# A float32 column sum: all loads but the first moved to the gpsimd queue, with shrinking tiles and a left-then-right end

## The chip, the cores and the metric

The kernel runs on one core of a Trainium2 chip. The metric is the device time of one execution in microseconds. Executions of one kernel beside each other lie within 0.3% here (630.0 to 630.8 us for the kernel before); only `tail_only` spreads by 0.5% (639.4 to 642.3 us). So differences of 2 us or more are safe here, and differences below 1 us are only called a tie or a tendency.

The engines are called as in the profile: PE is the tensor engine (PEld its weight loads), DVE the vector engine, ACT the scalar engine, POOL the gpsimd engine, SP the sync engine. A "queue" is the engine that issues a load. Loads issued by SP show up in the profile as `hardware_dynamic`, loads issued by POOL as `software_dynamic`.

## The reference

```python
# grad_output: (32, 1024, 2048) float32
def reference(grad_output):
    return np.sum(grad_output, axis=(0, 1)).astype(np.float32)     # 2048 sums over 32768 rows
```

The input is 268.4 MB and is read once. Below, a "row" is a slab of 128x2048 floats (1 MiB, one input row in each of the 128 partitions); there are 256 of them.

## The kernel before

31 tiles of 8 rows are loaded into three buffers. DVE folds each tile in halves (8 rows to 4 to 2 to 1) and adds the result to `acc`. The last 8 rows go into one more tile of the same three buffers, in pieces, and are not folded: PE multiplies them, and also `acc`, with a column of ones, which sums over the partitions into PSUM. The 2048 columns are cut into five pieces; the third number of a piece picks PSUM rows 0, 32, 64 or 96, called its row group here.

```python
ROWS = 8
TAIL = (4, 2, 1)
PIECES = ((0, 512, 1), (512, 512, 2), (1024, 512, 3), (1536, 256, 0), (1792, 256, 0))
# ... pools: io_pool with bufs=3, one tile of 128 x 8*2048 floats each; ones; acc ...
    for b, (lo, n, g) in enumerate(PIECES):
        bank = psum_pool.tile([P, 512], fp32, tag=f"ps{b}", name=f"ps{b}")
        sums.append(bank[32 * g : 32 * g + 1, :n])
# ...
    for t in range(n_bulk):                                   # 31 tiles
        T = io_pool.tile([P, ROWS * D], fp32, tag="T", name=f"t{t}")
        nc.sync.dma_start(out=T[:], in_=src)
        n = ROWS * D // 2
        while n >= D:                                         # 8 -> 4 -> 2 -> 1 rows
            # (the last step of tile 0 writes acc)
            nc.vector.tensor_add(out=T[:, :n], in0=T[:, :n], in1=T[:, n : 2 * n])
            n //= 2
        if t:
            nc.vector.tensor_add(out=acc[:], in0=acc[:], in1=T[:, :D])
    T = io_pool.tile([P, ROWS * D], fp32, tag="T", name="tail")
    for i, m in enumerate(TAIL):                              # 4, 2, 1 rows, then matmuls
        nc.sync.dma_start(out=T[:, at * D : (at + m) * D], in_=src)
        # ... add_row(...) for each of the m rows
    add_row(acc[:])
    for b, (lo, n, g) in enumerate(PIECES):                   # the last row, in five loads
        nc.sync.dma_start(out=dst, in_=flat[row : row + P, lo : lo + n])
        add_piece(b, dst, stop=True)
        # copy sums[b] to res: ACT for b = 0, 2, 4, DVE for b = 1, 3
    nc.sync.dma_start(out=out[None, :], in_=res)
```

The instruction streams are not simply this text. The build puts each engine's instructions in an order of its own, as the data dependencies allow.

## Time and profile before

| | before |
|---|---|
| time, median of 3 (630.2 us of 4 in the result below) | 630.1 us |
| span of the profiled run | 628.2 us |
| DMA: share of 16 engines' span | 99.0% |
| DVE busy | 87% |
| adds of one 8-row tile | 8.69 + 4.43 + 2.29 + 2.29 = 17.7 us |
| from tile to tile | 19.4 us |
| first adds start | 22.6 us |

From the profile page of the kernel before: the DMA share in 40 slices of the span, the rate in the same slices, and the queue.

```profile
DMA  9999999999999999999999999999999999999996
GB/s 401 413 455 401 467 401 467 401 467 401 467 401 467 401 467 401 463 405 459 409 459 409 455 413 455 413 455 413 451 417 451 417 446 421 438 430 426 442 403 266
q1 hardware_dynamic: 5618, 268.45, 99.0%
```

The DMA engines are busy in every slice but part of the last. (The rates swing because a packet, of which one of 64 KB takes 2.43 us on the mean in this trace, is counted whole in the slice where it starts.) This kernel is bound by its loads.

The groups of DVE instructions, kept apart by shape: count, total busy us, mean ns, and the idle time before them.

```profile
L67 DVE TENSOR_TENSOR t<-t 128x8192 f32<-128x8192 f32 x31 | 269.5, 8692 | 71.8 <-DMA t<-in_grad_output_dram 71.8
L67 DVE TENSOR_TENSOR t<-t 128x4096 f32<-128x4096 f32 x31 | 137.2, 4425 | 1.1
L70 DVE TENSOR_TENSOR acc<-acc,t 128x2048 f32<-128x2048 f32 x30 | 68.8, 2292 | 1.0
```

DVE waits for a load before every tile (71.8 us in all). The timeline of DVE at the start: start us, duration us, instructions (merged where they follow on).

```profile
22.61 13.15 DVE L67 TENSOR_TENSOR t<-t 128x8192 f32<-128x8192 f32 x2 [21.76 <-DMA t<-in_grad_output_dram]
35.80 2.29 DVE L65 TENSOR_TENSOR acc<-t 128x2048 f32<-128x2048 f32 x1
41.97 15.48 DVE L67 TENSOR_TENSOR t<-t 128x8192 f32<-128x8192 f32 x3 [3.88 <-DMA t<-in_grad_output_dram]
```

Tile 0 is folded from 22.6 to 38.1 us, and its buffer is then free for the fourth load. The three loads issued at the start keep the DMA engines busy until about 60.9 us, where their last packets end in the trace (their first packets start at 1.8 us). So the fourth load has over 20 us to spare.

The end, in windows of half a microsecond (the columns are busy us of PE, PEld, DVE, ACT, POOL, then clock, DMA share, GB/s), and the last wait for a landing, the copies and the store in the timeline:

```profile
622.00:622.50 0.50, 0.50 (x13) 0.26 (x9) 0.24 (x1) 0.00 (x0) 0.00 (x0) 1.00 1.06 361
622.50:623.00 0.50, 0.50 (x13) 0.26 (x8) 0.00 (x0) 0.00 (x0) 0.00 (x0) 1.00 0.57 182
623.00:623.50 0.50, 0.50 (x11) 0.09 (x2) 0.00 (x0) 0.00 (x0) 0.00 (x0) 1.00 0.07 25
```
```profile
624.20 0.20 PEld L49 LDWEIGHTS ps<-tail,ones 128*1 128x1 f32 x2 [0.24 <-DMA tail<-in_grad_output_dram]
624.34 1.57 ACT L89 COPY acc<-ps 1x512 f32<-1x512 f32 x3 [622.12 <-PE ps L49]
624.38 1.13 DVE L91 COPY acc<-ps 1x512 f32<-1x512 f32 x2 [2.14 <-PE ps L49]
625.93 0.33 SPq L92 DMA_DIRECT2D out_dram<-acc  x1
```

Traffic, counted where packets start, ends at about 622.7 us, the three ACT copies run one after another, and the store ends the span at 628.2: 5.5 us after 622.7.

### The profile page before, as it was taken

To read this page: it belongs to the slowest core of one execution; us is meant where nothing else is said; L and a number is where in the kernel's file an instruction comes from. 1 tells how busy PE (TensorE), PEld (TensorE's weight loads), DVE (VectorE), ACT (ScalarE), POOL (GpSimd) and SP (SyncE) were. 2 spreads that over 40 slices of the span, in tenths; PEclk is the share of its full clock that TensorE was granted. 3 is DMA by queue.
4 is the path that set the end of the run, shared out by engine and by line. 5 is a ranking of instruction groups with operands and counts; after the bars stand their busy time and mean duration, and the time that the engine had idled before them with its cause. 6 is when DMAs were issued, how large, how long until landed. Compare 5 with 4: busy or idle time off the path is not lost.

```text
span 628.2 us, 430 instructions
## 1 busy us (share of the span) xinstructions
PE 10.6 (2%) x90; PEld 3.8 (1%) x90; DVE 547.6 (87%) x126; ACT 3.0 (0%) x5; POOL 0.2 (0%) x4
## 2 busy tenths in 40 slices
PE   0000000000000000000000000000000000000006
PEld 0000000000000000000000000000000000000002
DVE  0578988889888899888898888988889988899886
ACT  0000000000000000000000000000000000000000
POOL 0000000000000000000000000000000000000000
PEclk9999999999999999999999999999999999999999
DMA  9999999999999999999999999999999999999996
GB/s 401 413 455 401 467 401 467 401 467 401 467 401 467 401 467 401 463 405 459 409 459 409 455 413 455 413 455 413 451 417 451 417 446 421 438 430 426 442 403 266
DMA packets 5619, 268.45 MB, mean 427 GB/s; under 512 B 625, under 2 KB 881, under 8 KB 1265
## 3 DMA queue, kind: packets, MB, share of 16 engines
q1 hardware_dynamic: 5618, 268.45, 99.0%
q14 instruction: 1, 0.01, 0.0%
HBM read 268.44 MB, written 0.01 MB: 427 GB/s over the span
## 4 chain that ended last, share of the span: by engine, by line
DMA 69%; DVE 28%; PE 2%; issue 0%; ACT 0%; SPq 0%; ACTq 0%
DMA t<-in_grad_output_dram 64%; DVE t L67 25%; DMA tail<-in_grad_output_dram 5%; DVE acc L70 4%; PE ps L49 2%; ACT acc L89 0%; SPq L60 0%; ACTq L118 0%
## 5 line engine op out<-in xcount | busy, mean ns | idle before, releaser
L67 DVE TENSOR_TENSOR t<-t 128x8192 f32<-128x8192 f32 (+2 forms) x92 | 475.4, 5167 | 73.9 <-DMA t<-in_grad_output_dram 71.8
L70 DVE TENSOR_TENSOR acc<-acc,t 128x2048 f32<-128x2048 f32 x30 | 68.8, 2292 | 1.0
L49 PE MATMUL ps<-tail,ones 128*1 128x512 f32 (+1 forms) x80 | 10.0, 627 | 614.3 <-DMA tail<-in_grad_output_dram 614.3
L49 PEld LDWEIGHTS ps<-tail,ones 128*1 128x1 f32 x80 | 3.5, 97 | 620.3 <-issue 617.4
L89 ACT COPY acc<-ps 1x512 f32<-1x512 f32 (+1 forms) x3 | 1.5, 506 | 622.2 <-PE ps L49 622.1
L91 DVE COPY acc<-ps 1x512 f32<-1x512 f32 (+1 forms) x2 | 1.1, 548 | 2.2 <-PE ps L49 2.1
L65 DVE TENSOR_TENSOR acc<-t 128x2048 f32<-128x2048 f32 x1 | 2.3, 2292 | 0.0
L39 ACT ACT_TABLE_LOAD x1 | 1.3, 1283 | 0.7 <-PEq L107 0.7
L49 PE MATMUL ps<-acc,ones 128*1 128x512 f32 (+1 forms) x10 | 1.1, 507 | 0.0
L37 DVE MEMSET ones<- 128x1 f32 x1 | 0.1, 59 | 0.8 <-PEq L107 0.8
L49 PEld LDWEIGHTS ps<-acc,ones 128*1 128x1 f32 x10 | 0.4, 82 | 0.4 <-DVE acc L70 0.2
L39 ACT COPY warm<-ones 1x1 f32<-1x1 f32 x1 | 0.2, 190 | 0.0
L107 POOL MEMSET const-bfloat16-1.0<- 128x1 bf16 x1 | 0.1, 101 | 0.0
L107 POOL MEMSET const-uint8-127<- 128x1 uint8 x1 | 0.1, 101 | 0.0
L107 POOL MEMSET const-float32-0.0<- 128x1 f32 x1 | 0.1, 98 | 0.2 <-issue 0.2
L107 POOL MEMSET const-float32-1.0<- 128x1 f32 x1 | 0.1, 98 | 0.0
## 6 DMA issues: line engine op xcount, KB each, us to landing
tail<-in_grad_output_dram SPq DMA_DIRECT2D x1, 4096.0 KB
tail<-in_grad_output_dram SPq DMA_DIRECT2D x1, 2048.0 KB, 35.1
tail<-in_grad_output_dram SPq DMA_DIRECT2D x1, 1024.0 KB, 37.1
tail<-in_grad_output_dram SPq DMA_DIRECT2D x3, 256.0 KB, 37.5
t<-in_grad_output_dram SPq DMA_DIRECT2D x31, 40.2
tail<-in_grad_output_dram SPq DMA_DIRECT2D x2, 128.0 KB, 28.6
out_dram<-acc SPq DMA_DIRECT2D x1, 8.0 KB
```

Source lines behind the costliest of these rows:

```text
L37: nc.vector.memset(ones[:], 1.0)
L39: nc.scalar.copy(out=warm[:], in_=ones[0:1, :])
L49: nc.tensor.matmul(sums[b], lhsT=ones[:], rhs=src, start=(b not in started), stop=stop)
L65: nc.vector.tensor_add(out=acc[:], in0=T[:, :n], in1=T[:, n : 2 * n])
L67: nc.vector.tensor_add(out=T[:, :n], in0=T[:, :n], in1=T[:, n : 2 * n])
L70: nc.vector.tensor_add(out=acc[:], in0=acc[:], in1=T[:, :D])
L89: nc.scalar.copy(out=res[:, lo : lo + n], in_=sums[b])
L91: nc.vector.tensor_copy(out=res[:, lo : lo + n], in_=sums[b])
L107: nc = _bacc.Bacc("TRN2", target_bir_lowering=False, num_devices=1)
```

## The change

It does five things. All loads but the first are issued by POOL. The tiles shrink at the end (26 of 8 rows, then 7, 7, 6, 6, 5, 5, 4, 2), so that little folding is left when the last bytes land. Six rows instead of eight go straight to PE: three whole ones and the last three. The last three rows are loaded as a left part (1536 columns) and then a right part (512 columns), so that the left part can be multiplied and copied while the right part is in flight. The piece at column 1792 moves to another row group. The diff, cut to its core:

```diff
-ROWS = 8
-TAIL = (4, 2, 1)
-PIECES = ((0, 512, 1), (512, 512, 2), (1024, 512, 3), (1536, 256, 0), (1792, 256, 0))
+FOLDED = (8,) * 26 + (7, 7, 6, 6, 5, 5, 4, 2)
+DIRECT = (3,)
+LAST = 3
+LEFT = ((0, 512, 1), (512, 512, 2), (1024, 512, 3))
+RIGHT = ((1536, 256, 0), (1792, 256, 1))
 ...
+    def load(m, lo=0, hi=D, at=None, advance=True, queue=None):
 ...
+            at = io_pool.tile([P, 8 * D], fp32, tag="T", name=f"t{row}_{lo}")[:, : m * n]
 ...
+        (queue or nc.gpsimd).dma_start(out=at.rearrange("p (m d) -> p m d", m=m), in_=src)
 ...
+    for i, m in enumerate(FOLDED):
+        T = load(m, queue=nc.sync if i == 0 else None)
+        while m > 1:
+            h = m // 2
+            into = acc[:] if i == 0 and m == 2 else T[:, : h * D]
+            nc.vector.tensor_add(out=into, in0=T[:, : h * D], in1=T[:, (m - h) * D : m * D])
+            m -= h
+        if i:
             nc.vector.tensor_add(out=acc[:], in0=acc[:], in1=T[:, :D])
+    for m in DIRECT:
+        T = load(m)
         for j in range(m):
+            add(T[:, j * D : (j + 1) * D], LEFT + RIGHT)
+    add(acc[:], LEFT + RIGHT)
+    T = io_pool.tile([P, 8 * D], fp32, tag="T", name="last")
 ...
+    for lo, hi, into in ((0, cut, left), (cut, D, right)):
+        row = first
+        for m in (LAST - 1, 1):
+            S = load(m, lo, hi, T[:, at : at + m * n])
 ...
+    for j, S in enumerate(left):
+        add(S, LEFT, stop=j == LAST - 1)
+    for j, S in enumerate(right):
+        add(S, RIGHT, base=cut, stop=j == LAST - 1)
```

More of the change, by code (lines that the diff above doesn't have):

```diff
@@ L28 @@
     R = flat.shape[0]
-    n_bulk = (R // P - sum(TAIL) - 1) // ROWS
-    assert (n_bulk * ROWS + sum(TAIL) + 1) * P == R
+    assert (sum(FOLDED) + sum(DIRECT) + LAST) * P == R
     io_pool = ctx.enter_context(tc.tile_pool(name="io", bufs=3))
@@ L40 @@
     acc = const_pool.tile([P, D], fp32)
-    sums = []
-    for b, (lo, n, g) in enumerate(PIECES):
+    sums = {}
+    for b, (lo, n, g) in enumerate(LEFT + RIGHT):
         bank = psum_pool.tile([P, 512], fp32, tag=f"ps{b}", name=f"ps{b}")
-        sums.append(bank[32 * g : 32 * g + 1, :n])
+        sums[lo] = bank[32 * g : 32 * g + 1, :n]
     started = set()
-    def add_piece(b, src, stop=False):
-        nc.tensor.matmul(sums[b], lhsT=ones[:], rhs=src, start=(b not in started), stop=stop)
-        started.add(b)
@@ L52, in add_row @@
-    def add_row(src):
-        for b, (lo, n, g) in enumerate(PIECES):
-            add_piece(b, src[:, lo : lo + n])
-    row = 0
-    for t in range(n_bulk):
-        T = io_pool.tile([P, ROWS * D], fp32, tag="T", name=f"t{t}")
-        src = flat[row : row + P * ROWS].rearrange("(p m) d -> p (m d)", p=P)
-        nc.sync.dma_start(out=T[:], in_=src)
-        row += P * ROWS
-        n = ROWS * D // 2
-        while n >= D:
-            if t == 0 and n == D:
-                nc.vector.tensor_add(out=acc[:], in0=T[:, :n], in1=T[:, n : 2 * n])
-            else:
-                nc.vector.tensor_add(out=T[:, :n], in0=T[:, :n], in1=T[:, n : 2 * n])
-            n //= 2
-        if t:
-            nc.vector.tensor_add(out=acc[:], in0=acc[:], in1=T[:, :D])
@@ L72, with add @@
-    T = io_pool.tile([P, ROWS * D], fp32, tag="T", name="tail")
-    at = 0
-    for i, m in enumerate(TAIL):
-        src = flat[row : row + P * m].rearrange("(p m) d -> p (m d)", p=P)
-        nc.sync.dma_start(out=T[:, at * D : (at + m) * D], in_=src)
-        row += P * m
-        for j in range(m):
-            add_row(T[:, (at + j) * D : (at + j + 1) * D])
-        at += m
-    add_row(acc[:])
-    res = acc[0:1, :]
-    for b, (lo, n, g) in enumerate(PIECES):
-        dst = T[:, at * D + lo : at * D + lo + n]
-        nc.sync.dma_start(out=dst, in_=flat[row : row + P, lo : lo + n])
-        add_piece(b, dst, stop=True)
-        if b in (0, 2, 4):
-            nc.scalar.copy(out=res[:, lo : lo + n], in_=sums[b])
+    def add(src, pieces, base=0, stop=False):
+        for lo, n, g in pieces:
+            nc.tensor.matmul(
+                sums[lo], lhsT=ones[:], rhs=src[:, lo - base : lo - base + n],
+                start=(lo not in started), stop=stop,
+            )
+            started.add(lo)
@@ new lines @@
+    row = 0
+    def load(m, lo=0, hi=D, at=None, advance=True, queue=None):
+        nonlocal row
+        n = hi - lo
+        if at is None:
+            at = io_pool.tile([P, 8 * D], fp32, tag="T", name=f"t{row}_{lo}")[:, : m * n]
+        src = flat[row : row + P * m].rearrange("(p m) d -> p m d", p=P)[:, :, lo:hi]
+        (queue or nc.gpsimd).dma_start(out=at.rearrange("p (m d) -> p m d", m=m), in_=src)
+        if advance:
+            row += P * m
+        return at
+    for i, m in enumerate(FOLDED):
[6 more added lines that the diff above has]
+        if i:
+            nc.vector.tensor_add(out=acc[:], in0=acc[:], in1=T[:, :D])
@@ new lines @@
+    for m in DIRECT:
+        T = load(m)
+        for j in range(m):
+            add(T[:, j * D : (j + 1) * D], LEFT + RIGHT)
+    add(acc[:], LEFT + RIGHT)
+    T = io_pool.tile([P, 8 * D], fp32, tag="T", name="last")
+    cut, at, left, right = RIGHT[0][0], 0, [], []
+    first = row
+    for lo, hi, into in ((0, cut, left), (cut, D, right)):
+        row = first
+        for m in (LAST - 1, 1):
+            n = hi - lo
+            S = load(m, lo, hi, T[:, at : at + m * n])
+            into += [S[:, j * n : (j + 1) * n] for j in range(m)]
+            at += m * n
@@ L90 @@
+    for j, S in enumerate(left):
+        add(S, LEFT, stop=j == LAST - 1)
+    for j, S in enumerate(right):
+        add(S, RIGHT, base=cut, stop=j == LAST - 1)
+    res = acc[0:1, :]
+    for k, (lo, n, g) in enumerate(LEFT + RIGHT):
+        if k in (0, 2, 4):
+            nc.scalar.copy(out=res[:, lo : lo + n], in_=sums[lo])
         else:
-            nc.vector.tensor_copy(out=res[:, lo : lo + n], in_=sums[b])
+            nc.vector.tensor_copy(out=res[:, lo : lo + n], in_=sums[lo])
     nc.sync.dma_start(out=out[None, :], in_=res)
```

## The prediction

> **What bounds it now.** The loads. On the page the DMA digit is 9 in 39 of 40 slices, and the queue list gives one hardware queue 99.0% of the 16 engines' span, 268.45 MB, 427 GB/s over the span. The vector engine is 87% busy, but waits for a load before every tile (71.8 us in 31 waits). Steady state: an 8-row tile lands about every 19.4 us (432 GB/s, 2.43 us per row of 128x2048); its adds take 8.69 + 4.43 + 2.29 + 2.29 = 17.7 us. With three buffers a load is issued when the tile three back is added up; about 20 us of transfers are still queued then, so the queue never runs dry.
>
> Edges: transfers begin near 1.2 us; the first load lands at 22.6, about 2 us after its bytes should be through. At the end (small windows) traffic dies at 622.7, the last pieces are seen by 624.2, ACT copies three pieces in series to 625.9, the store ends at 628.2: 5.5 us after the last bytes.
>
> **What the change does.**
> 1. Bytes unchanged, so about 621 us of transfers stay. All loads but the first move to the software queue. [...]I expect the same 432 GB/s within 1%.
> 2. At the start the first load (SP) and the second (gpsimd) share the engines. I expect the first to land near 40 us, not 22.6, so the adds start some 18 us late. The fourth load is issued about 57 us, just before the queue empties (59.5): a bubble of 0 to 2 us. The vector engine regains 1.6 us per tile and is level well before the end.
> 3. Shrinking tiles empty the queue. With 5, 4, 2, 3, 3 rows at the end, the last tile needs the buffer of the 4-row tile. The built order shows the final add of that tile behind the first add of the 2-row tile. From the last byte of the second 5-row load: it lands at 1.9, its adds end at 13.2, those of the 4-row tile (the 2-row add ahead) at 24.6. Transfers of 4, 2 and 3 rows end by about 22. [...]so the last 3 rows start near 26: a bubble of about 4 us, absent before.
> 4. Left-then-right: the first 1536 columns are multiplied and copied while the right part is in flight; after the last landing only two matmuls and one copy: 0.5 to 1 us saved.
>
> [...]
>
> **Sum.** 630.1 + 4 (late bubble) + 0.5 (early) - 0.7 (end) = about 633.5 us. Range 626 to 641. Faster by over 2%: 0.02; within: 0.90; slower: 0.08.
>
> **What shows it right.** Chain: near the end, an add of the 2- and 4-row tiles releases the gpsimd issue of the last tile, and windows there show 3 to 5 us of low GB/s. First vector add near 40 us. Tiles spaced 19.4 us. Last landing to span end 5 us or less. Wrong if the DMA share stays full to the end, or the first add starts at 22.6.
>
> **What would make it wrong.** A software queue that moves bytes slower (each 1% is 6 us) or faster; [...]issue latency of several us.

## The result, and the profile after

The changed kernel takes 644.1 us (median of 4 runs, 643.6 to 644.6) against 630.2 us. The ratio is 1.0219 (95% interval 1.0202 to 1.0237), so it is slower by a little over 2%. A ratio here is the mean time of one kernel's fast runs over that of the other's of the same rounds, so it is not quite the ratio of the medians quoted. The spans of the profiled runs differ by 642.2 - 628.2 = 14.0 us, and that is what has to be explained.

The page of the changed kernel:

```profile
DMA  9997799999999999999999999999999999999995
GB/s 392 457 392 327 327 392 457 453 396 457 412 437 457 392 457 445 404 453 441 412 453 400 453 453 396 457 453 396 453 445 408 453 404 454 413 432 444 430 367 196
q0 software_dynamic: 5536, 260.05, 94.1%
q1 hardware_dynamic: 146, 8.40, 3.1%
```

The DMA share has a dent in the fourth and fifth slices, 48 to 80 us. Between that dent and the end the rate is as before: 433 GB/s from 90 to 544 us in the changed kernel, 433 GB/s from 61.5 to 585 us in the kernel before.

**The early gap.** The timeline at the start of the changed kernel:

```profile
39.52 25.96 DVE L78 TENSOR_TENSOR t<-t 128x8192 f32<-128x8192 f32 x4 [38.65 <-DMA t<-in_grad_output_dram]
65.40 2.28 DVE L78 TENSOR_TENSOR acc<-t 128x2048 f32<-128x2048 f32 x1
67.97 0.53 POOL L68 DMA_DIRECT2D t<-in_grad_output_dram  x1 [65.53 <-DVE acc L78]
...
90.13 15.48 DVE L78 TENSOR_TENSOR t<-t 128x8192 f32<-128x8192 f32 x3 [0.46 <-DMA t<-in_grad_output_dram]
```

The first adds start at 39.5 us, as predicted, because the first two loads share the engines: from 7.3 to 34.3 us packets of both queues start in the trace, at 419 GB/s in all from 20 to 30 us. They land at 39.5 and 41.9 us. But then DVE does four adds in a row before the one that finishes tile 0. The built instruction order of the vector engine says which: the 128x8192 add of tile 0, the same of tile 1, the 128x4096 add of tile 0, the same of tile 1, and only then the add of tile 0 into `acc`. So tile 0's buffer comes free after 8.69 + 8.69 + 4.43 + 4.43 + 2.28 = 28.5 us of adds instead of 15.4, and the fourth load is issued at 67.97 us instead of about 55. The window from 58.5 to 69 us, first in the kernel before, then in the changed one:

```profile
58.50:69.00 10.50, 0.00 (x0) 0.00 (x0) 8.76 (x2) 0.00 (x0) 0.00 (x0) 1.00 1.00 424
```
```profile
58.50:69.00 10.50, 0.00 (x0) 0.00 (x0) 10.50 (x4) 0.00 (x0) 0.53 (x1) 1.00 0.00 0
```

No packet starts in that window. (The third load's last packets, begun by 58.5 us, end at 60.9; the next packet starts at 69.2, so the DMA engines stand still for 8.3 us.) The adds of the fourth tile start at 90.13 us against 81.06 before: 9.1 us are lost, and they are never regained, because the loads are what bounds the kernel.

**The late gap.** The end of the chain of waits of the changed kernel (start us, us, what):

```profile
616.03 4.35 DVE t L78
620.38 0.02 issue
620.41 4.49 DVE t L78 x2
624.90 2.21 DVE acc L81
627.11 0.28 issue
627.40 1.25 POOL last L68 x2
628.64 9.28 DMA last<-in_grad_output_dram
```

These are the adds of the 4-row tile, with the first add of the 2-row tile among them; they end at 627.11, and only then does POOL issue the last loads. The windows of the changed kernel there:

```profile
625.00:626.00 1.00, 0.00 (x0) 0.00 (x0) 1.00 (x1) 0.00 (x0) 0.00 (x0) 1.00 0.35 148
626.00:627.00 1.00, 0.14 (x4) 0.13 (x8) 1.00 (x1) 0.00 (x0) 0.00 (x0) 1.00 0.00 0
627.00:628.00 1.00, 1.00 (x8) 0.13 (x1) 0.97 (x2) 0.00 (x0) 0.60 (x1) 1.00 0.00 0
628.00:629.00 1.00, 1.00 (x9) 0.18 (x8) 1.00 (x1) 0.00 (x0) 1.00 (x3) 1.00 0.73 80
629.00:630.00 1.00, 1.00 (x9) 0.21 (x2) 0.43 (x1) 0.00 (x0) 0.92 (x2) 1.00 0.59 123
```

From 625.3 to 629.6 us the rate is 49 GB/s. That is the predicted gap of about 4 us.

**The sum.** Traffic ends at about 637.7 us, against 622.7: 15.0 us later. Of these 9.1 are the early gap, so 5.9 are lost late: (432 - 49)/432 x 4.3 = 3.8 us in the gap, and the rest in a smaller dip near 618 us and in the last pieces, which run at 367 GB/s. From the end of traffic to the end of the span it is 4.5 us instead of 5.5, so 1.0 us is saved there; the run `after_g0` below shows by what. 9.1 + 5.9 - 1.0 = 14.0 us.

### The profile page after: what moved, and what is told of

Read it like the earlier page. It is cut to its first block, busy times and chain, and to the rows that moved or that the text cites. A ratio compares the mean times of both kernels' runs of the same rounds, so it can differ in the third digit from the quotient of the medians.

```text
span 642.2 us, 404 instructions
## 1 busy us (share of the span) xinstructions
PE 12.1 (2%) x70; PEld 2.8 (0%) x70; DVE 551.9 (86%) x135; ACT 3.0 (0%) x5; POOL 20.8 (3%) x42
## 4 chain that ended last, share of the span: by engine, by line
DMA 60%; DVE 34%; issue 5%; PE 0%; POOL 0%; POOLq 0%
DMA t<-in_grad_output_dram 59%; DVE t L78 29%; DVE acc L81 5%; DMA last<-in_grad_output_dram 1%; PE ps L54 0%; POOL last L68 0%; DVE acc L108 0%; POOLq L68 0%
## 5 line engine op out<-in xcount | busy, mean ns | idle before, releaser
L78 DVE TENSOR_TENSOR t<-t 128x2048 f32<-128x2048 f32 (+3 forms) x98 | 473.7, 4838 | 76.8 <-DMA t<-in_grad_output_dram 74.7
L81 DVE TENSOR_TENSOR acc<-acc,t 128x2048 f32<-128x2048 f32 x33 | 75.6, 2291 | 1.1
L68 POOL DMA_DIRECT2D t<-in_grad_output_dram x34 | 18.1, 532 | 598.3 <-DVE acc L81 532.0
L54 PE MATMUL ps<-t,ones 128*1 128x512 f32 (+1 forms) x30 | 6.6, 807 | 626.9 <-DMA t<-in_grad_output_dram 626.9
L54 PE MATMUL ps<-last,ones 128*1 128x512 f32 (+1 forms) x30 | 4.5, 506 | 0.4 <-DMA last<-in_grad_output_dram 0.3
L54 PEld LDWEIGHTS ps<-t,ones 128*1 128x1 f32 x30 | 1.3, 96 | 631.7 <-issue 631.7
L68 POOL DMA_DIRECT2D last<-in_grad_output_dram x4 | 2.5, 637 | 10.5 <-DVE acc L81 10.5
## 6 DMA issues: line engine op xcount, KB each, us to landing
t<-in_grad_output_dram POOLq DMA_DIRECT2D x1, 2048.0 KB, 13.7
```

The costliest lines, as they stand in the source:

```text
L54: nc.tensor.matmul(sums[lo], lhsT=ones[:], rhs=src[:, lo - base : lo - base + n], start=(lo not in started), stop=stop,)
L68: (queue or nc.gpsimd).dma_start(out=at.rearrange("p (m d) -> p m d", m=m), in_=src)
L78: nc.vector.tensor_add(out=into, in0=T[:, : h * D], in1=T[:, (m - h) * D : m * D])
```

## The experiments

The theory: the loss is two stops of the loads, each because a buffer is freed late. The whole of the early one needs two things together, namely that the first two loads on different queues land at nearly the same time (2.4 us apart), and that the build then interleaves their adds. The late one comes from the buffers of the shrinking tiles. Rival A: two queues at once lose bandwidth. Rival B: the software queue is slow, or what POOL does to issue a load is held up by the adds. Each run has runs of the kernel before beside it on the same chip (their medians are 629.6 to 629.8 us), and its ratio is against those. The changed kernel's 644.1 us were measured beside a kernel before at 630.2 us, so where another run's time is subtracted from 644.1, up to about 0.6 us of the difference can be that.

### Repairing the two gaps

`order_only` keeps the queues and forces the adds of tiles 0 to 4 to go tile by tile, with a one-column add (0.16 us) that reads `acc` and the next tile, so that this tile's adds cannot start sooner:

```diff
         T = load(m, queue=nc.sync if i == 0 else None)
+        if 1 <= i <= 4:
+            nc.vector.tensor_add(out=order[:], in0=acc[:, :1], in1=T[:, :1])
```

> Queues as in the change; four one-column adds force the tile-by-tile order of the adds at the start. Theory (the build interleaved the adds of tiles 0 and 1, so the first buffer came free at 67.7 us instead of 55 and the queue ran dry for 9 us): first adds still start near 39.5, the fourth load is issued near 55 us and lands near 81 instead of 90, time about 635 us. Rival A (two queues at once lose bandwidth at the start): still about 644. Rival B (software queue slow[...]): still about 644.

Measured: 634.4 us (ratio 1.0072, 1.0055 to 1.0089). The first adds of this run, and the next issue of a load:

```profile
39.84 13.15 DVE L81 TENSOR_TENSOR t<-t 128x8192 f32<-128x8192 f32 x2 [38.97 <-DMA t<-in_grad_output_dram]
53.03 2.29 DVE L81 TENSOR_TENSOR acc<-t 128x2048 f32<-128x2048 f32 x1
```
```profile
55.61 0.53 POOL L69 DMA_DIRECT2D t<-in_grad_output_dram  x1 [53.17 <-DVE order L77]
```

The first load still lands late, at 39.8 us (and the second at about 42.2, an estimate from the 2.4 us between them in the changed kernel), but the fourth load is issued at 55.6 us instead of 68.0, the window from 59 to 69 us now carries 419 GB/s, and 9.7 us are gone. Rival A predicted no gain and falls.

`tail_only` keeps the interleaving and puts all rows after the 4-row tile into one buffer, so that nothing waits for the adds of the 4-row tile any more:

```diff
-FOLDED = (8,) * 26 + (7, 7, 6, 6, 5, 5, 4, 2)
-DIRECT = (3,)
+FOLDED = (8,) * 26 + (7, 7, 6, 6, 5, 5, 4)
+DIRECT = (2, 3)                    # these and the last 3 rows: one tile T, loaded piece by piece
```

> Queues and interleaving as in the change; the rows after the 4-row tile (2, 3 and the last 3) go into one buffer, so the last loads no longer wait for the adds of the 4-row tile. Theory: no gap of traffic near the end, early gap stays, about 639.5 us (4 to 5 us less than the change). Rival B: the late gap is the slow issue of small software loads, so it stays: about 644.

Measured: 640.6 us, but with the widest spread (639.4 to 642.3), ratio 1.0174. The late gap is gone: 421 GB/s from 605 to 625 us. The gain is 3.5 us, less than the 4 to 5 expected.

`order_and_tail` has both edits.

> Both repairs, loads still on the software queue except the first. Theory: the two gaps are separate and add up to all of the loss, so about 630 us (629 to 631.5), level with the kernel before. Rival B: 640 or more.

Measured: 631.6 us (ratio 1.0025, 1.001 to 1.004). Of the 14 us, 12 are back with 97% of the bytes still on the software queue. The remaining 1.9 us missed the expectation, and are taken up below.

`all_gpsimd` only moves the first load to POOL as well.

```diff
-        T = load(m, queue=nc.sync if i == 0 else None)
+        T = load(m, queue=None)
```

> The change with the first load on the software queue too. Theory: loads then land one after the other (first near 23 us), the build keeps tile order, no early gap; the late gap stays: about 635 us. Rival A: the same, about 635 (it does not tell A apart; order_only does). Rival B: as slow as the change or slower, 644 or more.

Measured: 635.2 us (ratio 1.0086). More of the work on the software queue makes the kernel 8.9 us faster: with one queue the loads land one after the other (first adds at 23.7 us), and the build keeps the adds in tile order. Rival B falls for the early gap.

### Each part of the change alone, and the order alone

`before_mixed` is the kernel before with only the queues changed: the first load on SP, all others on POOL.

```diff
-        nc.sync.dma_start(out=T[:], in_=src)
+        (nc.gpsimd if t else nc.sync).dma_start(out=T[:], in_=src)
 ...   # and nc.gpsimd for the loads of the tail
```

> The kernel before, with only the queue part of the change: first load on SP, all others from gpsimd, tile sizes and end untouched. Theory: the built order interleaves tiles 0 and 1 here too, so the early gap of 9 us comes with the queue alone: first adds at 39.5, about 639 us (638 to 640.5). If the early gap came from the shrinking sizes or the new end instead: about 630 to 631.

Measured: 639.0 us (ratio 1.0148): 9.3 us for a change of queue names. Its built order interleaves too, and the fourth load is issued at 67.9 us.

`before_gpsimd` puts all its loads on POOL.

> The kernel before with every load from gpsimd: tile order as before. Theory: only the later start of the software queue is lost, about 1 us at the start, the same 19.4 us per 8-row tile: about 631 us (630.5 to 632). Rival B (a slower software queue[...]): 634 or more.

Measured: 630.5 us (ratio 1.0015, 1.0000 to 1.0030). The start of the same late tile shows the pace. First the kernel before, whose second tile started at 41.97 us, then `before_gpsimd`, whose second tile started at 42.71 us:

```profile
565.73 8.69 DVE L67 TENSOR_TENSOR t<-t 128x8192 f32<-128x8192 f32 x1 [1.53 <-DMA t<-in_grad_output_dram]
```
```profile
566.21 8.69 DVE L67 TENSOR_TENSOR t<-t 128x8192 f32<-128x8192 f32 x1 [1.54 <-DMA t<-in_grad_output_dram]
```

27 tiles later: (565.73 - 41.97)/27 = 19.40 us per tile on the hardware queue, (566.21 - 42.71)/27 = 19.39 on the software queue. The software queue costs its later start, 0.7 us at the second tile, and nothing per byte.

`gpsimd_interleaved` has all loads on POOL, so that no two queues share the engines, but writes the adds of tiles 0 and 1 in the interleaved order, held there by two one-column adds:

```diff
+    A, B = load(8), load(8)
+    half(A, 8); half(B, 8)
+    nc.vector.tensor_add(out=order[:], in0=A[:, :1], in1=B[:, :1])
+    half(A, 4); half(B, 4)
+    nc.vector.tensor_add(out=order[:], in0=A[:, :1], in1=B[:, :1])
+    nc.vector.tensor_add(out=acc[:], in0=A[:, :D], in1=A[:, D : 2 * D])
+    half(B, 2)
+    nc.vector.tensor_add(out=acc[:], in0=acc[:], in1=B[:, :D])
```

> All loads from gpsimd (no two queues at once), but the adds of tiles 0 and 1 written in the interleaved order of the changed kernel. Theory: the order alone frees the first buffer only near 63 us (tile 1 lands at 43, then 8.7 + 4.4 + 4.4 + 2.3 us of adds), the queue is dry from 60.6, so a gap of about 4 us: about 639 us against 635.2 for the same queues without it. Rival A (two queues at once are the cause): 635.

Measured: 638.9 us (ratio 1.0146) against 635.2. In its timeline the second tile's add sits in front of the rest of the first tile's:

```profile
23.45 8.69 DVE L76 TENSOR_TENSOR t<-t 128x8192 f32<-128x8192 f32 x1 [22.59 <-DMA t<-in_grad_output_dram]
42.78 8.69 DVE L76 TENSOR_TENSOR t<-t 128x8192 f32<-128x8192 f32 x1 [10.64 <-DMA t<-in_grad_output_dram]
```
```profile
63.03 0.53 POOL L69 DMA_DIRECT2D t<-in_grad_output_dram  x1 [60.06 <-DVE order L84]
```

So the order alone costs 3.7 us, two loads landing together cost nothing alone (`order_only` has them, and is as fast as `all_gpsimd`), and both together cost 9 us.

`all_sync` is the change with every load on SP: the sizes and the end alone.

```diff
-        (queue or nc.gpsimd).dma_start(
+        nc.sync.dma_start(
```

> The change with every load from SP. Theory: no early gap, the late gap stays because it comes from the buffers, [...]and the start is 1 us earlier than from gpsimd: about 633 us. Rival B (the queue is the cause of the loss): 630 or less.

Measured: 634.0 us (ratio 1.0067). The first adds start at 22.6 us, against 23.7 in `all_gpsimd`. The late gap is there on the hardware queue as well: no packet starts from 616.2 to 618.2 us. The queues alone cost 9.3 us and the sizes and the end alone 4.4 us, and 9.3 + 4.4 = 13.7 us is nearly the whole loss.

### What the repair still lost

In `tail_only` and `order_and_tail` the matmuls finished late. In the profile of `order_and_tail` they paused for 2.3 us and restarted under a lower granted clock:

```profile
616.20:618.20 2.00, 1.60 (x14) 0.47 (x17) 0.00 (x0) 0.00 (x0) 0.00 (x0) 0.78 1.04 427
618.20:620.20 2.00, 2.00 (x14) 0.30 (x9) 0.00 (x0) 0.00 (x0) 0.00 (x0) 0.50 0.99 406
...
622.20:624.20 2.00, 2.00 (x18) 0.49 (x14) 0.00 (x0) 0.00 (x0) 0.00 (x0) 1.00 0.31 117
624.20:626.20 2.00, 2.00 (x19) 0.45 (x15) 0.00 (x0) 0.00 (x0) 0.00 (x0) 1.00 0.00 0
```

My first explanation was this clock (the column before the DMA share). Three runs load the last eight rows as 4, 2, 1 and a last row in two parts, so that the matmuls do not pause; two of them were also to beat the kernel before, with all loads on SP.

```diff
-DIRECT = (2, 3)
-LAST = 3
+DIRECT = (4, 2, 1)
+LAST = 1                           # loaded as 1536 and 512 columns
```

`order_and_421` is `order_and_tail` with this edit. `sync_short_421` is the same with all loads on SP and no ordering adds. `sync_eights_421` is `sync_short_421` with `FOLDED = (8,) * 31`.

> order_and_tail, with the eight rows after the 4-row tile loaded as 4, 2, 1 and a last row in two parts (1536 and 512 columns) instead of 2, 3 and 3 in four parts. Theory: the 1.9 us that order_and_tail still lost is the matmuls, which restarted after 2 us without work at a granted clock of 0.5 and finished 2.6 us late; with 4, 2, 1 they run without a break as in the kernel before, so about 630 us, level with before within 0.1%. If the 1.9 us came from the queue or the loads: still about 631.6.

> The version that should be best: all loads from SP, sizes shrinking from 8 to 4, the last eight rows in one buffer as 4, 2, 1 and a last row in two parts. The transfers (about 621 us) stay; only the matmuls and copies after the last landing shrink: 0.5 to 1 us under the kernel before, about 629 us.

> The same end, but the folded loads stay 8 rows (the kernel before, with only the left-then-right end). If the shrinking sizes matter at the end (the last tile's adds finish just before the last landing), this is 0.3 to 0.8 us slower than sync_short_421, about 629.7; if only the left-then-right end matters, equal to it.

Measured: 633.5, 633.3 and 633.3 us (ratios 1.0054, 1.0064 and 1.0056): slower than `order_and_tail`, with a granted clock of 1.00 in all windows of the matmuls. The pause and the low clock after it were gone and the loss was larger, so these versions lose by something else. That does not clear the clock in `order_and_tail`. Nor does a column of 1.00 prove full pace: in `sync_eights_421` it reads 1.00 from the first matmul on, but 13 matmul records lie in the window from 615.5 to 617.5 us and 20 in that from 619.5 to 621.5 us, with PE busy throughout both. `sync_eights_421` is nearly the kernel before, yet its matmuls end about 3 us later. The last two rows in its timeline (`acc`, then the last loaded row), then those in the kernel before:

```profile
624.74 0.60 PE L54 MATMUL ps<-acc,ones 128*1 128x512 f32 x3
...
626.03 0.60 PE L54 MATMUL ps<-last,ones 128*1 128x512 f32 x3
```
```profile
622.42 1.05 PE L49 MATMUL ps<-acc,ones 128*1 128x512 f32 x10
623.28 1.63 PE L49 MATMUL ps<-tail,ones 128*1 128x512 f32 x10
```

From one row to the next it is 626.03 - 624.74 = 1.29 us, and 0.86 us in the kernel before: a ratio of 1.5. That points to a part of the diff that I had passed over. The piece at column 1792 moved from row group 0 to row group 1, so group 1 now has 512 + 256 = 768 of a row's columns, where before every group had 512; 768/512 is 1.5. My estimate from these figures: matmuls of one group follow one another and those of different groups overlap, so that a row takes as long as its fullest group. Four more runs undo only this:

```diff
-RIGHT = ((1536, 256, 0), (1792, 256, 1))
+RIGHT = ((1536, 256, 0), (1792, 256, 0))
```

> order_and_tail with the piece at column 1792 back in row group 0. New theory (matmuls of one group follow one another, those of different groups overlap, so a row takes as long as its fullest group: 0.86 us per row at 512 columns, 1.29 at 768): the nine rows are done when the last piece lands, about 630 us, within 0.1% of before. If the low granted clock is the cause after all: still about 631.5.

> sync_short_421 with the piece at column 1792 in row group 0. New theory: 0.86 us per row once warm, matmuls level with the loads, copies of the left part done early: about 629.2 us, 0.3 to 0.8 us under before. If the group is not the cause: still 633.3.

> sync_eights_421 with the same repair: what is left is the kernel before with its last row in two parts instead of five. New theory: 629.0 to 629.8 us, at most 0.6 us under before. If the group is not the cause: still 633.3.

> The change itself with only the group repaired. Its matmuls have 6 to 7 us of gap in the traffic to catch up in, so nothing should be gained: 643.5 to 644.3 us. If the group cost anything in the change: 642.5 or less.

| run | without the edit | with it | ratio to before, with it |
|---|---|---|---|
| `order_and_tail_g0` | 631.6 | 630.7 | 1.0015 (1.0000 to 1.0031) |
| `sync_short_421_g0` | 633.3 | 630.7 | 1.0012 (0.9999 to 1.0024) |
| `sync_eights_421_g0` | 633.3 | 630.0 | 1.0002 (0.9989 to 1.0014) |
| `after_g0` | 644.1 | 645.0 | 1.0241 (1.0227 to 1.0255) |

All four missed what was expected of them, the first three by 0.2 to 1.5 us. Still, the group was the cause in the 4, 2, 1 versions: in `sync_eights_421_g0` the last two rows are again 0.86 us apart (622.23 and 623.09 us in its timeline). In `order_and_tail` undoing it gains 0.9 us, about half of the 1.9 us, and that is a tendency only; the other half, about 1 us, is not explained by a run of its own. Two things point to the clock for it. In `order_and_tail_g0` the matmuls pause for 3.6 us, and after that three rows (30 matmul records) run at half pace, though the clock column reads 1.00:

```profile
616.23 4.98 PE L55 MATMUL ps<-last,ones 128*1 128x512 f32 x30 [3.63 <-DMA last<-in_grad_output_dram]
```

That is 1.7 us per row, much as at their first start (20 records, two rows, in 3.59 us), while the `acc` row after them takes 0.86 us (621.03 to 621.89 us). And the record gives the mean granted clock of each execution: `order_and_tail` took 630.2 us at 1.000 and 631.4 to 631.9 us at 0.997 (three executions); `tail_only` took 639.4 and 639.9 us at 1.000, 641.4 us at 0.997 and 642.3 us at 0.995. No run changes the clock alone, so that it costs this time is not shown.

`after_g0` missed its expectation, and usefully. In the change itself the uneven groups gain about 1 us (the two were measured in different sessions, but the traces show it), since at its very end only the two right pieces are multiplied, and those are in different groups. The timelines of the changed kernel and of `after_g0` after the last landing:

```profile
637.96 1.46 PE L54 MATMUL ps<-last,ones 128*1 128x256 f32 x12 [0.31 <-DMA last<-in_grad_output_dram]
```
```profile
638.07 2.75 PE L54 MATMUL ps<-last,ones 128*1 128x256 f32 x12 [0.28 <-DMA last<-in_grad_output_dram]
```

So the choice of group helps the end (1.46 us against 2.75) and hurts every whole row (1.29 us against 0.86). In the change the end is what counts; in the repaired kernels the whole rows are.

No version beat the kernel before; `sync_eights_421_g0` ties with it. Of the 628.2 us of span about 621 are transfers (268.4 MB at 432 GB/s, an estimate from the pace of the tiles), so an end that is shorter by 1 us can win 0.2% at most.

## Why the prediction was wrong

The predicted time was 633.5 us, with a range of 626 to 641, and the chance of slower by over 2% was put at 0.08. Measured were 644.1 us and slower by 2.2%. Point by point:

1. *What bounds the kernel, and the rate of the software queue* ("the same 432 GB/s within 1%"): right. 433 GB/s in the long middle of both, and 19.39 against 19.40 us per tile in `before_gpsimd`.
2. *The early bubble* ("the fourth load is issued about 57 us ... a bubble of 0 to 2 us"): this is the step that failed. The first half was right (the first load lands near 40 us; measured 39.5). The second half assumed that DVE would finish tile 0 before it touched tile 1, as in the kernel before. The built program interleaves them, the fourth load is issued at 67.97 us, and the bubble is 9.1 us. (The queue emptied at 60.9 us and not at 59.5, so an issue at 57 us would have been in time.) `order_only`, which changes only that order, gives 9.7 us back; `before_mixed`, which has only the queues, loses 9.3 us. The built instruction order was there to be read before the prediction. I read its end, where the 2-row tile's add stands inside the 4-row tile's, and took the start for granted.
3. *The late bubble* ("about 4 us"): mechanism and gap right. The chain of waits shows the adds of the 4- and 2-row tiles before the issue of the last tile, and traffic is down to 49 GB/s for 4.3 us. The step from the end of the adds to the start of the last loads (24.6 to near 26 on the prediction's scale) was my estimate; measured were 1.7 us, from 627.11 us to the first packet at 628.81. The sum was undersized: the traffic loses 5.9 us late, because of a second small dip and the slower last pieces, which I left out. With the saving at the end, `order_only` and `all_sync` put this part at 4.4 to 4.6 us net, where the prediction had 4 - 0.7 = 3.3.
4. *The left-then-right end* ("0.5 to 1 us saved"): the number came out, 1.0 us counted from where traffic ends (0.4 us counted from the end of the last packet, at 623.7 and 638.1 us), but by luck. After the last landing the prediction had two matmuls and one copy; the trace has 12 matmul records (six matmuls of the program) and two copies. Counted from the last landing that PE waits for, the end takes 642.2 - 637.96 = 4.2 us, and 628.2 - 624.20 = 4.0 us in the kernel before. In `after_g0`, with the piece at column 1792 back in its old group, it takes 643.5 - 638.07 = 5.4 us. So it was the moved piece that kept the end short, and the prediction does not mention it. `sync_eights_421_g0`, the kernel before with a last row loaded left then right, gains nothing.
5. *POOL's issues under the adds*: not held up. The issue at 67.97 us ran under adds and took 0.53 us, like almost all the others (the first two, before any add ran, took 1.20 us together), and the tiles kept their pace of 19.4 us.
6. *What would make it wrong*: I named a software queue of another rate and an issue latency of several us. Neither came: 19.39 us per tile in `before_gpsimd`, and 0.28 us from the end of the adds to POOL's issue in the chain above. The thin slack at the start tore by another way, the order of the adds.

With 9.1 us in place of 0.5 for step 2 the sum is 630.1 + 4 + 9.1 - 0.7 = 642.5 us, close to the measured time; the 1.6 us that remain are the undersized step 3.

## What to carry to other kernels

When loads bound a kernel, ask of each buffer which instruction frees it, and read in the built order where that instruction stands; changing only the issuing queue of a load can reorder the compute engine's work and delay the next loads (9.3 us in `before_mixed`). Splitting the first loads over two queues delivered the first late and the second no earlier here (39.5 and 41.9 us, against 22.6 and 41.9; by itself this cost nothing, see `order_only`), and in a ring of three buffers the first to be done is what keeps the loads going. Shrinking tiles at the end also shrink the transfers that cover a buffer's release (traffic fell to 49 GB/s for 4.3 us here), so the last small loads should go into a buffer that is already free.

## Further figures from the traces

- Two 8.4 MB loads on two queues landed at 39.5 and 41.9 us in the changed kernel, and on one queue, in the kernel before, at 22.6 and 41.9 us. With the order that the build then chose, `before_mixed` lost 9.3 us.
- The first adds started 0.75 us later in `before_gpsimd` than in the kernel before (23.36 against 22.61 us), of which 0.5 us is that POOL issued later (1.25 against 0.73 us). The delay from a released buffer to the issue on POOL was 0.28 us in the chain above.
- A 2048-column row took 0.86 us with 512 columns in each of four groups (`before`, `sync_eights_421_g0`), and 1.29 us with 768 in one of them (`sync_eights_421`).
- The clock column turned to 0.50 at 617.3 us in `order_and_tail`, 0.7 us after the matmuls restarted from a pause of 2.3 us, and stayed there for 3.4 us. In `tail_only` it turned at 627.2 us, 1.1 us after the restart from a pause of 2.1 us, also for 3.4 us. (These times are worked out from the means of windows of 1 us.) What sets them is not tested by any run here.
- Where the clock column reads 1.00 the pace can still differ. In the kernel before the matmuls of 512 columns took 1049 ns on the mean from 614 to 617 us (1061 at most) and 592 ns in the `acc` row from 622.4 us; in `order_and_tail_g0` three rows ran at half pace after the pause of 3.6 us.
